# Two transformer blocks in one program: order of the first loads, halves of the output products, the router's choice, and the tail

## The chip, the cores and the metric

The kernel runs on one core of one Trainium2 chip. The metric is the device time of one execution in microseconds (us). Before the change three runs took 1857.16 us in the median (1853.68 to 1857.87).

## The reference

The program computes two blocks on 256 tokens of width 1024, all in fp32. `norm` is a root-mean-square norm, `ln` a layer norm.

```python
# first block
h = x
h = h + rglru_and_forgetting_attention(norm(h))       # w_in -> u, gate, q, k, v, f ; w_out
h = h + cross_attention(norm(h), norm(mem))           # 4 heads of 256, memory of 256
h = h + relu(norm(h) @ w_up) ** 2 @ w_down            # 1024 -> 4096 -> 1024
h = h + dilated_and_sliding_window_attention(norm(h)) # w_in -> qc, kc, vc, qd, kd, vd ; w_out
h = h + cross_attention(norm(h), norm(mem))
h = h + relu(norm(h) @ w_up) ** 2 @ w_down
x = norm(h)
# second block, twice (i = 0: f is latent attention, i = 1: f is a pooling mixer)
x = ln(a * x + f(x))
x = ln(a * x + moe(x))
# moe: the best of 8 groups of experts per token, in it the best 2 of 8 experts, gates by softmax
#   expert e: (silu(t @ w1[e]) * (t @ w3[e])) @ w2[e],  1024 -> 256 -> 1024, 64 experts
```

The kernel reads the weights of all 64 experts in both MoE layers (3 MB for each expert).

## The kernel before

**Products.** A product of the first block runs as three matmuls: both sides are split into a high part (`wh`, `yh`, by ScalarE) and a low part (`wl`, `yl`, by VectorE), and high·high, high·low and low·high are summed in PSUM. `split_steps` (L231, L234) splits a weight tile, `hilo` (L331, L332) an activation, `transposed` (L341 to L347) transposes x on TensorE and splits it on the way out of PSUM. `g_feat` (L301) makes a product by features: `mid` is called after its first weight half, `end` after its second, and `step` runs one step of the background work `bg` inside. `g_out` (L317) makes the products with an output matrix into four PSUM banks, for the token blocks b = 0 and 1.

**Weights.** All weights come over SyncE's queue (SP) in one list of items of about 1 MB, into a ring of buffers (13 more join for the MoE). `issue` starts loads as far ahead as the ring is free, `w` takes the next item and splits two further on, `tick` splits one half tile inside attention loops. Transfers of SP's queue run on eight lanes: a load waits for the one eight before it. The order of all other work is the order in which the Python text is executed; each engine works its queue in this order.

**First mixer (`mixer0`).** x is loaded by two DMAs, transposed, and multiplied to "u", "gate", then "vf", "kv" and so on. The row sums' scale `rs` (L356 to L372) is made in the middle of "u"; the products are multiplied by it as they leave PSUM (`evac`, L556). The recurrence `lru` is background work. Its small matrices `bd` come by four POOL DMAs (L551), `bf` by another (L540). `memory_start` transposes the memory (L341, L347).

**Attention.** `attend.main` loops over pairs of heads p: transposes of the probabilities (L470, L472), softmax of pair p+1, scores of p+2 (L712), `tick`, the output products of the pair before (`outp(p - 1)`, L317), the product with the values `pv` (L481) and its `hilo`. `cross` has a loop of the same form over four heads. `outl` is the output product of the recurrence's half.

**MoE (`moe`).** The choice of experts needs the logits `L` (L1318, L1322), two maxima with their indices (L1334, L1336), 0/1 masks `M` and counts by a triangular product (L1358). A gather (L1416) then builds the rows of four experts; `up` multiplies by w1 and w3 (L1452), `turned` transposes, `down` multiplies by w2 (L1481) and adds into the result by a gate matrix (L1490, `out`). 16 groups of four experts follow one another; w1, w3 and w2 of one expert are three items of 1 MB.

**End.** The last group (layer 1, group 15) takes w2 in four tiles of 256 columns for all four experts (`last`, L1511, L1504). `last_gain` broadcasts the final gain and bias (L1008), `finish` does the layer norm (L1023 to L1036) and the output (L1681, L1684) and stores it (L1685).

## Time and profile before

| what | value |
|---|---|
| median of the runs shown | 1857.16 us (1853.68 to 1857.87) |
| profiled execution | 1854.02 us, its span 1852.2 us |
| TensorE (PE) busy | 1649.1 us, 89% of the span |
| VectorE (DVE) busy | 760.0 us, 41% |
| ScalarE (ACT) busy | 577.7 us, 31% |
| GpSimd (POOL) busy | 10.2 us, 1% |
| read from memory | 546.97 MB, 296 GB/s over the span |
| mean granted TensorE clock | 0.964 |

The span is the time between the first and the last instruction of the profiled execution; 1.8 us lie around it. A busy share is a mean over stages. The first block takes the first 640 us and more, the latent attention ends at about 908 us, and the two MoE layers fill the rest.

### The profile page before, as it was taken

The page shows a single profiled execution, that of the slowest core. Times are in us where ns is not written, and L with a number is a line of the kernel's source. Part 1 is how long each engine was busy: PE and PEld are TensorE (multiplying, and loading weights), DVE is VectorE, ACT ScalarE, POOL GpSimd, SP SyncE. Part 2 cuts the span into 40 slices and gives each one's busy share as a digit, 9 for nine tenths or more (in the row PEclk, how much of TensorE's full clock was granted, in tenths as well). Part 3 has the DMA queues.
Part 4 walks back from the last instruction along what each step waited for, and adds up shares of the span by engine and source line. Part 5 has one row for each costly group of instructions (what it writes and reads, how often), then busy time and mean ns, then how long its engine had stood idle before and what let it go on. Part 6 is the DMA issues. An engine that isn't in the chain of part 4 may idle for free.

```text
span 1852.2 us, 29897 instructions
## 1 busy us (share of the span) xinstructions
PE 1649.1 (89%) x12712; PEld 1196.5 (65%) x12712; DVE 760.0 (41%) x1599; ACT 577.7 (31%) x1047; POOL 10.2 (1%) x22
## 2 busy tenths in 40 slices
...
GB/s 290 182 160 117 134 162 203 182 184 180 182 114 129 117 180 189 183 152 259 307 387 425 426 427 424 425 425 427 422 424 418 426 426 427 426 424 426 426 427 234
DMA packets 127842, 550.10 MB, mean 297 GB/s; under 512 B 9660, under 2 KB 33551, under 8 KB 78927
## 3 DMA queue, kind: packets, MB, share of 16 engines
...
q10 hardware_dynamic: 144, 0.21, 0.0%
HBM read 546.97 MB, written 1.05 MB: 296 GB/s over the span
## 4 chain that ended last, share of the span: by engine, by line
PE 54%; DMA 40%; DVE 3%; ACT 3%; issue 1%; SPq 0%; DVEq 0%; ACTq 0%
DMA wr<-in_moe_w 38%; PE a L317 16%; PE b L301 9%; PE a L301 4%; PE b L1452 4%; PE a L280 3%; PE b L741 3%; PE b L1416 2%; PE a L741 2%; DMA wr<-in_ab_w_in 1%; PE a L1490 1%; PE b L1481 1%; PE b L481 1%; PE b L470 1%; DVE wl L234 1%
## 5 line engine op out<-in xcount | busy, mean ns | idle before, releaser
L1452 PE MATMUL b<-wr,xg 128*32 128x256 f32 x4096 | 306.2, 422 | 111.2 <-DMA wr<-in_moe_w 108.9
L234 DVE TENSOR_TENSOR wl<-wr,wh 128x1024 fp32r<-128x1024 f32 (+4 forms) x268 | 309.5, 1197 | 120.8 <-ACT wh L231 77.2
L1452 PEld LDWEIGHTS b<-wr,xg 128*32 128x32 f32 x4096 | 145.0, 121 | 278.1 <-DMA wr<-in_moe_w 148.1
L231 ACT ACTIVATE wh<-wr 128x1024 fp32r<-128x1024 f32 (+4 forms) x268 | 265.1, 1037 | 106.4 <-DVE wl L234 72.4
L1457 DVE SCALAR_TENSOR_TENSOR th<-th,b 128x256 f32<-128x256 f32 x32 | 13.5, 421 | 487.2 <-ACT th L1456 487.2
L317 PE MATMUL a<-wh,yh 128*128 128x512 f32 x416 | 168.0, 404 | 2.7 <-ACT yh L331 2.7
L1456 ACT ACTIVATE th<-b 128x256 f32<-128x256 f32 x32 | 12.3, 383 | 506.3 <-PE b L1452 506.3
L317 PE MATMUL a<-wh,yl 128*128 128x512 f32 x416 | 165.1, 397 | 0.6 <-DVE yl L332 0.6
L317 PE MATMUL a<-wl,yh 128*128 128x512 f32 x416 | 164.1, 394 | 0.0
L1481 PE MATMUL b<-wr,hT 128*32 128x512 f32 x992 | 124.9, 603 | 28.8 <-ACT hT L1468 22.3
L1416 PE MATMUL b<-G,x 128*128 128x128 f32 x1024 | 130.0, 287 | 19.6 <-DVE G L1398 10.6
L1416 PEld LDWEIGHTS b<-G,x 128*128 128x128 f32 x1024 | 123.5, 200 | 33.1 <-issue 17.9
L301 PE MATMUL b<-xh,wl 128*128 128x256 f32 x448 | 121.9, 282 | 0.0
L301 PE MATMUL b<-xh,wh 128*128 128x256 f32 x448 | 121.7, 281 | 0.0
L1490 PE MATMUL a<-Y,GT 128*128 128x512 f32 x248 | 117.2, 615 | 0.0
L301 PE MATMUL b<-xl,wh 128*128 128x256 f32 x448 | 110.3, 282 | 0.0
L1481 PEld LDWEIGHTS b<-wr,hT 128*32 128x32 f32 x992 | 32.1, 110 | 100.7 <-issue 54.8
L317 PEld LDWEIGHTS a<-wh,yh 128*128 128x128 f32 x416 | 78.1, 188 | 23.3 <-ACT yh L331 4.5
L317 PEld LDWEIGHTS a<-wh,yl 128*128 128x128 f32 x416 | 78.1, 188 | 22.5 <-DVE yl L332 3.9
L1490 PEld LDWEIGHTS a<-Y,GT 128*128 128x128 f32 x248 | 42.0, 189 | 74.6 <-issue 30.5
L301 PE MATMUL a<-xh,wh 128*128 128x256 f32 x320 | 88.4, 286 | 1.3 <-ACT xh L345 0.9
L317 PEld LDWEIGHTS a<-wl,yh 128*128 128x128 f32 x416 | 78.2, 188 | 17.3
...
## 6 DMA issues: line engine op xcount, KB each, us to landing
wr<-in_moe_w SPq DMA_DIRECT2D x372, 1024.0 KB, 19.6
...
```

The lines of the kernel that those rows point to most:

```text
L231: nc.scalar.activation(hi[:, s], r[:, s], AF.Copy)
L234: nc.vector.tensor_tensor(lo[:, s], r[:, s], hi[:, s].bitcast(F32), op=ALU.subtract)
L280: nc.tensor.matmul(outs[b][j], xT(a, h * 4 + kk)[:, b * 128:(b + 1) * 128], wt[c][:, kk, j * n:(j + 1) * n], start=(h == 0 and kk == 0 and ...
L301: nc.tensor.matmul(o[f // 2][:, f % 2, :], wt[c][:, kk, f * 128:(f + 1) * 128], xT(a, h * 4 + kk), start=(h == 0 and kk == 0 and a == 0 an ...
L317: nc.tensor.matmul(acc[b][hf], yT[a][:, chunk, b * 128:(b + 1) * 128], wt[c][:, j, hf * 512:(hf + 1) * 512], start=(first and a == 0 and c ...
L470: nc.tensor.transpose(ps[:, o:o + 128], s[:, o:o + 128], self.ident)
L481: nc.tensor.matmul(o[r, sl], V(2 * p + e, kb), PT[p][e][:, 256 * kb:256 + 128 * kb], start=(kb == 0), stop=(kb == 1))
L741: nc.tensor.matmul(o[:, f], lt, rt, start=(k == 0 and f == 0 and a == 0 and c == 0), stop=(k == 7 and c == 1), skip_group_check=True)
L1416: nc.tensor.matmul(ps[:, k], xk[:, b, 4 * i + k], Gf[:, b], start=(b == 0), stop=(b == 1))
L1452: nc.tensor.matmul(ps[32 * e:32 * e + 32, which], xg[:, k, 32 * e:32 * e + 32], w(e, k), start=(which == 0 and k == 0), stop=(k == 7), ski ...
L1481: nc.tensor.matmul(y[hf][32 * e:32 * e + 32], hT[:, c, 32 * e:32 * e + 32], w(c)[:, hf * 512:(hf + 1) * 512], start=(c == 0), stop=(c == 1 ...
L1490: nc.tensor.matmul(acc[b][hf], GT[:, b * 128:(b + 1) * 128], Y[:, hf * 512:(hf + 1) * 512], start=first, stop=end, skip_group_check=True)
```

## The change

It has four parts.

1. Start: x comes in two halves of columns, the first weights between them; the rows of small vectors and the identity come over ScalarE's queue. `bf` and `bd` are loaded on SP, after the small vectors and ahead of the memory. The transposes of x are made in two parts, the second inside "u". `rs` is made at the end of "u", and its broadcast, the evacuation of u and the start of `lru` stand in the middle of "gate" (`scales`).
2. Output products: of the last pair, block 0's stand ahead of `pv` and block 1's behind it; the same by halves in `cross` and for `outl`; in the second mixer `turn("qd")` moves into the first pair.
3. Router: x is copied by ScalarE and VectorE, the expert is chosen in one 64-wide maximum over masked logits, the 0/1 matrices are bf16, and the first group gathers all rows ahead of its products, the gates ahead of them and the counts behind.
4. Tail: w3 of the last group comes in tiles of two experts by half of the rows, w2 in two tiles of two experts by 512 columns and two of four experts by 256; `last_gain` moves ahead by a group in layer 1; `finish` is divided over three engines.

```diff
         if self.w_split <= i or not self.attending:
-            self.split(i + (1 if i < 3 else 3 if key == ("lat", 1) else 2))
+            self.split(i + (0 if i == 0 else 1 if i < 3 else 3 if key == ("lat", 1) else 2))
...
+    def g_out(self, yT, chunk, wt, j, acc, first, last, blocks=(0, 1)):
         nc = self.nc
-        for b in range(2):
+        for b in blocks:
             for hf in range(2):
...
-                if p:
+                if p == n - 1:
+                    outp(p - 1, (0,))
+                elif p:
                     outp(p - 1)
                 elif pend:
                     pend()
                 if p == 0 and nxt:
                     follow = nxt()
                 pv(p)
+                if p == n - 1:
+                    outp(p - 1, (1,))
                 self.step()
...
-            xT = self.norm_in(R_AB, first)
+            xT = self.xt()
+            self.transposed(x, R_AB, xT, first, range(4))
+            for _ in first:
+                pass
+
+            def rest():
+                self.transposed(x, R_AB, xT, ks=range(4, 8))
+                yield
+            self.bg.append(rest())
...
-            nc.gpsimd.dma_start(bf, A["fox_b_f"].to_broadcast([128, 8]))
+            nc.sync.dma_start(bf, A["fox_b_f"].to_broadcast([128, 8]))
...
-                    nc.gpsimd.dma_start(bd[64 * e:64 * e + 64, i, :, 64 * e:64 * e + 64],
+                    nc.sync.dma_start(bd[64 * e:64 * e + 64, i, :, 64 * e:64 * e + 64],
...
-            o = self.g_feat(xT, "u", mid=lambda: self.rstd(x, None, out=rs))
-            rb, rbq = self.rbc(rs, (1.0, -0.125), "ab")
-            evac(upad[:, :, 3:259], o, rb)
-            self.bg.append(lru())
-            self.g_feat(xT, "gate", end=lambda o: evac(gate, o, rb))
+            ou = self.g_feat(xT, "u", end=lambda o: self.rstd(x, None, out=rs))
+            rbs = []
+
+            def scales():
+                rbs.extend(self.rbc(rs, (1.0, -0.125), "ab"))
+                evac(upad[:, :, 3:259], ou, rbs[0])
+                self.bg.append(lru())
+            self.g_feat(xT, "gate", mid=scales, end=lambda o: evac(gate, o, rbs[0]))
+            rb, rbq = rbs
...
-                if p % 2 == 0:
+            def outp(p, blocks=(0, 1)):
+                if p % 2 == 0 and 0 in blocks:
                     self.wo = self.w("ab_of", p // 2)
-                self.g_out(yb, p, self.wo, p % 2, acc, False, p == 3)
-
-            def outl(i):
-                wt = self.w("ab_ol", i)
-                for c in range(2):
-                    self.g_out(ya, 2 * i + c, wt, c, acc, i + c == 0, False)
-
-            outl(0)
-            last, _ = att.main(ahead=2)
-            outl(1)
+                self.g_out(yb, p, self.wo, p % 2, acc, False, p == 3, blocks)
+
+            def outl(i, c):
+                if c == 0:
+                    self.wl = self.w("ab_ol", i)
+                self.g_out(ya, 2 * i + c, self.wl, c, acc, i + c == 0, False)
+
+            outl(0, 0)
+            last, _ = att.main(pend=lambda: outl(0, 1), ahead=2)
+            outl(1, 0)
+            outl(1, 1)
             last()
             self.residual(x, acc)
...
                 self.tick(2)
                 if h:
-                    outp(h - 1)
+                    outp(h - 1, 0)
                 self.tick(2)
                 pv(h)
+                if h:
+                    outp(h - 1, 1)
             self.attending = False
             if before_last:
                 before_last()
-            outp(3)
+            outp(3, 0)
+            outp(3, 1)
             self.residual(x, acc)
...
-                turn("qd")
                 att0.pro(1)
                 self.attend_on()
             proj("vc", 0, mid)
...
-            fin, att1 = att0.main(nxt=swa)
+            fin, att1 = att0.main(pend=lambda: turn("qd"), nxt=swa)
...
+        zo = wp.tile([128, 2, 128], F32, name="hT", bufs=1).bitcast(BF16)
+        utb, onb = zo[:, 0, :128], zo[:, 1, :128]
+        i64 = small("i64", 64)
+        nc.gpsimd.tensor_copy(utb, self.ut)
+        nc.gpsimd.tensor_copy(onb, self.ones)
+        for i in range(2):
+            nc.gpsimd.tensor_scalar(i64[:, 32 * i:32 * i + 32], iota, 32.0 * i - 1.0, None, op0=ALU.add)
+        st, mv, r, u, rs, nb = self.norm_tiles(wp)
         for b in range(2):
-            for h in range(2):
-                nc.scalar.activation(half_x(b, h), by8(y[b][h]), AF.Copy)
+            nc.scalar.activation(half_x(b, 0), by8(y[b][0]), AF.Copy)
+            nc.vector.tensor_copy(half_x(b, 1), by8(y[b][1]))
+            if b == 0:
+                nc.vector.bn_stats(st[:, 0, 0], y[0][0])
+        for b in range(2):
...
+        self.norm_scales(2, st, mv, r, u, rs, nb)
+        for b in range(2):
+            stt(L[:, b], ps[:, b], rs[:, b:b + 1], self.lbr[:, l], op0=ALU.mult, op1=ALU.add)
...
+        gm, gi = largest("g", gl)
+        ne = small("ne", 2, 8)
+        Lm, o2 = (wp.tile([128, 256], F32, name=n, bufs=1)[:, :128].rearrange("p (b n) -> p b n", b=2) for n in ("th", "h"))
+        stt(ne, io8, -1.0, gi[:, :, 0:1].to_broadcast([128, 2, 8]), op0=ALU.add, op1=ALU.not_equal)
         for b in range(2):
...
+            stt(Lm[:, b].rearrange("p (g e) -> p g e", g=8), ne[:, b, :, None].to_broadcast([128, 8, 8]), -BIG,
+                L[:, b, 8:72].rearrange("p (g e) -> p g e", g=8), op0=ALU.mult, op1=ALU.add)
+        em, ei = largest("e", Lm)
+        o1 = small("o1", 2, 64)
+        M = wp.tile([128, 2, 64], BF16, name="r_M")
+        for j, o in enumerate((o1, o2)):
+            tt(o, i64[:, None, :].to_broadcast([128, 2, 64]), ei[:, :, j:j + 1].to_broadcast([128, 2, 64]), op=ALU.is_equal)
+        tt(M, o1, o2, op=ALU.add)
...
                     for e in range(4):
-                        it.append(((n, l, g, e), w[l, 4 * g + e].rearrange("(p k) f -> p k f", k=8), (8, 256)))
+                        if (l, g, n) == (1, 15, 3):
+                            it.append(((n, l, g, e), w[l, 4 * g + 2 * (e % 2):4 * g + 2 * (e % 2) + 2].rearrange(
+                                "e (p k) f -> p e k f", k=8)[:, :, 4 * (e // 2):4 * (e // 2) + 4], (2, 4, 256)))
...
-                        it.append(((2, l, g, e), A["moe_w2_2"][l, 4 * g:4 * g + 4].rearrange("e (p c) d -> p c e d", c=2)
-                                   [:, :, :, e * 256:(e + 1) * 256], (2, 4, 256)))
+                        es, ds = (slice(2 * e, 2 * e + 2), slice(0, 512)) if e < 2 else (slice(0, 4), slice(e * 256, (e + 1) * 256))
+                        it.append(((2, l, g, e), A["moe_w2_2"][l, 4 * g:4 * g + 4][es].rearrange("e (p c) d -> p c e d", c=2)
+                                   [:, :, :, ds], (2, es.stop - es.start, ds.stop - ds.start)))
...
+            def out(o, n):
+                for b in range(2):
+                    nc.tensor.matmul(acc[b][o // 512][:, o % 512:o % 512 + n], GT[:, b * 128:(b + 1) * 128],
+                                     Y[:, o:o + n], start=False, stop=True, skip_group_check=True)
+            wh = [self.raw_w(2, l, g, i) for i in range(2)]
+            hidden(0, 512, lambda c, e: wh[e // 2][:, c, e % 2])
+            for q in (2, 3):
+                w = self.raw_w(2, l, g, q)
+                hidden(q * 256, 256, lambda c, e: w[:, c, e])
+                out(*((0, 512) if q == 2 else (512, 256)))
+            out(768, 256)
...
-        Gg = []
-
-        def mid():
-            nonlocal G
-            gates()
-            half(1)
-            Gg.append(weighted(0, G))
-            G = slots(1, s1)
-        h = up(0, xg, parts(0), mid)
-        GT = back(Gg.pop())
+        half(1)
+        gates()
+        Gg = weighted(0, G)
+        G = slots(1, s1)
+        h = up(0, xg, parts(0))
+        rounds()
+        GT = back(Gg)
...
+            if g == 14 + (l == 0):
+                before_last()
             if g != OVER:
                 hT = turned(h)
             if 0 < g < 15:
                 GTn = back(Gg)
-            fill = []
-            if g == 15 and l == 0:
-                before_last()
-            if g == 14 and l == 1:
-                fill = [lambda i=i: before_last(i) for i in range(2)]
             if g != OVER:
-                down(g, hT, GT, acc, None if (l, g) == (1, 15) else w2g, g == 0, g == 15, fill)
+                down(g, hT, GT, acc, None if (l, g) == (1, 15) else w2g, g == 0, g == 15)
...
+        for j in range(4):
+            for b in range(2):
+                nc.vector.bn_stats(st[:, b, j], acc[b][j // 2][:, (j % 2) * 256:(j % 2 + 1) * 256])
+        self.norm_scales(4, st, mv, r, u, rs, nb)
+        o = [wp.tile([128, 1024], F32, name=n, bufs=1) for n in ("xg", "Y")]
+        h = slice(512, 1024)
+        nc.scalar.activation(o[1][:, h], acc[1][1], AF.Identity, scale=rs[:, 1:2], bias=nb[:, 1:2])
+        for i, op in ((0, ALU.mult), (1, ALU.add)):
+            nc.gpsimd.tensor_tensor(o[1][:, h], o[1][:, h], x[:, i, h], op=op)
+        for b, i in ((0, 0), (0, 1), (1, 0)):
+            s = slice(i * 512, (i + 1) * 512)
+            nc.vector.scalar_tensor_tensor(o[b][:, s], acc[b][i], mv[:, b, 0:1], x[:, 0, s], op0=ALU.subtract, op1=ALU.mult)
+            nc.vector.scalar_tensor_tensor(o[b][:, s], o[b][:, s], rs[:, b:b + 1], x[:, 1, s], op0=ALU.mult, op1=ALU.add)
+            nc.sync.dma_start(self.out[0, b * 128:(b + 1) * 128, s], o[b][:, s])
+        nc.scalar.dma_start(self.out[0, 128:, h], o[1][:, h])
...
-            nc.scalar.dma_start(keep, A["cst"][:, :C_KEEP])
-            nc.sync.dma_start(rows, A["rows"])
-            for b in range(2):
-                nc.sync.dma_start(x[:, b], A["x"][0, b * 128:(b + 1) * 128])
+
+            half = lambda h: nc.sync.dma_start(x[:, :, h * 512:(h + 1) * 512],
+                                               A["x"][0].rearrange("(b p) d -> p b d", p=128)[:, :, h * 512:(h + 1) * 512])
+            nc.scalar.dma_start(self.ident, A["cst"][:, C_ID:C_ID + 128])
+            nc.scalar.dma_start(rows, A["rows"])
+            half(0)
+            self.issue(0)
+            half(1)
+            self.issue(self.depth)
             nc.vector.memset(self.ones, 1.0)
             nc.scalar.activation(self.junk[:, :2], self.ones[:, :2], AF.Copy)
             nc.gpsimd.memset(self.brow, 0.0)
             nc.gpsimd.memset(self.bsrow, 0.0)
-            self.issue(1)
+            nc.sync.dma_start(keep[:, 128:], A["cst"][:, 128:C_KEEP])
             nc.sync.dma_start(cst, A["cst"][:, C_KEEP:])
-            self.issue(self.depth)
```

Three places show the order in the queues. VectorE's queue in the first products: `rb` is the broadcast scale, `upad` holds u, `wl` are the low parts of weights, `lc` begins the constants of the recurrence, `rs` is the scale. Before:

```order
L372 SCALAR_TENSOR_TENSOR rs<-nwt,nwy 128x2
L234 TENSOR_TENSOR wl<-wr,wh 128x1024 x2
L382 TENSOR_SCALAR rb_341<-b 128x256
L382 TENSOR_SCALAR rb_343<-b 128x256
L556 TENSOR_TENSOR upad<-a,rb_341 128x2x256 x2
L234 TENSOR_TENSOR wl<-wr,wh 128x1024 x2
L562 TENSOR_SCALAR lc<-col 128x8
```

and now:

```order
L377 SCALAR_TENSOR_TENSOR rs<-nwt,nwy 128x2
L239 TENSOR_TENSOR wl<-wr,wh 128x1024 x2
L387 TENSOR_SCALAR rb_400<-b 128x256
L387 TENSOR_SCALAR rb_402<-b 128x256
L573 TENSOR_TENSOR upad<-a,rb_400 128x2x256 x2
L579 TENSOR_SCALAR lc<-col 128x8
L414 SCALAR_TENSOR_TENSOR l1e<-col 128x4
```

The evacuation of u stood between the low parts of the first half of "gate" and those of its second; now it stands behind both. Four `wl` of 128x1024 (the second half of "u" and the first of "gate") stand ahead of the scale where two did.

TensorE's queue at the first group of layer 0, from the end of the triangular product on; `G` gathers, `xg` are the gathered rows, `r_M` the 0/1 matrix of the counts. (An fp32 product is counted once here and twice in the trace.) Before:

```order
L1358 MATMUL b<-r_M,keep 128x64
L1416 MATMUL b<-G,x 128x128 x8
L1452 MATMUL b<-wr,xg 32x256 x16
L1386 MATMUL b<-r_M,ones 128x64 x2
L1416 MATMUL b<-G,x 128x128 x8
L1452 MATMUL b<-wr,xg 32x256 x48
```

and now:

```order
L1411 MATMUL b<-r_M,hT 128x64
L1465 MATMUL b<-G,x 128x128 x16
L1497 MATMUL b<-wr,xg 32x256 x64
L1436 LDWEIGHTS hT
L1436 MATMUL b<-r_M,hT 128x64
```

The second half of the gather stood between the first 16 up products and the other 48; now the whole gather stands ahead of all 64, and the product of the counts behind them.

TensorE's queue at the end of the program, from the turn of the last group on. Before:

```order
L1466 MATMUL b<-keep,h 128x128 x2
L1511 MATMUL b<-wr_19715,hT 32x256 x8
L1511 MATMUL b<-wr_19718,hT 32x256 x8
L1504 MATMUL a<-Y,GT 128x256 x2
L1511 MATMUL b<-wr_19749,hT 32x256 x8
L1504 MATMUL a<-Y,GT 128x256 x4
L1511 MATMUL b<-wr_19752,hT 32x256 x8
L1504 MATMUL a<-Y,GT 128x256 x2
```

and now:

```order
L1510 MATMUL b<-keep,h 128x128 x2
L1544 MATMUL b<-wr_19698,hT 32x512 x2
L1544 MATMUL b<-wr_19701,hT 32x512 x2
L1544 MATMUL b<-wr_19698,hT 32x512 x2
L1544 MATMUL b<-wr_19701,hT 32x512 x2
L1544 MATMUL b<-wr_19732,hT 32x256 x8
L1550 MATMUL a<-Y,GT 128x512 x2
L1544 MATMUL b<-wr_19735,hT 32x256 x8
L1550 MATMUL a<-Y,GT 128x256 x4
```

The w2 products of the first 512 columns are now eight 512-wide ones over two tiles, and fewer output products (`Y`, `GT`) stand behind the last weights.

## Rows read from the trace of the kernel before

**Rows 1.** The page's slices of 46 us: what the DMA engines moved.
```profile
GB/s 290 182 160 117 134 162 203 182 184 180 182 114 129 117 180 189 183 152 259 307 387 425 426 427 424 425 425 427 422 424 418 426 426 427 426 424 426 426 427 234
```

**Rows 2.** The page's chain that ended last, by engine and line.
```profile
DMA wr<-in_moe_w 38%; PE a L317 16%; PE b L301 9%; PE a L301 4%; PE b L1452 4%; PE a L280 3%; PE b L741 3%; PE b L1416 2%; PE a L741 2%; DMA wr<-in_ab_w_in 1%; PE a L1490 1%; PE b L1481 1%; PE b L481 1%; PE b L470 1%; DVE wl L234 1%
```

**Rows 3.** Stretches: us, busy of PE, PEld, DVE, ACT, POOL, clock, DMA share, GB/s.
```profile
14.00:22.00 8.00, 7.71 (x62) 7.38 (x62) 7.43 (x16) 7.97 (x17) 0.00 (x0) 1.00 1.05 397
14.00:48.00 34.00, 31.88 (x252) 30.48 (x252) 31.31 (x76) 23.21 (x41) 0.00 (x0) 1.00 0.87 303
129.00:168.00 39.00, 37.62 (x223) 28.94 (x222) 25.19 (x85) 17.70 (x50) 0.00 (x0) 1.00 0.33 109
199.00:238.00 39.00, 37.45 (x180) 30.11 (x179) 18.15 (x29) 17.10 (x33) 0.00 (x0) 1.00 0.41 131
238.00:512.00 274.00, 273.74 (x1789) 248.65 (x1789) 169.50 (x235) 128.84 (x173) 1.25 (x2) 1.00 0.56 183
512.00:572.00 60.00, 58.71 (x348) 43.83 (x347) 40.35 (x144) 37.19 (x107) 0.00 (x0) 1.00 0.28 95
602.00:638.00 36.00, 34.53 (x158) 26.93 (x157) 16.34 (x23) 12.65 (x23) 0.00 (x0) 1.00 0.30 99
925.00:930.00 5.00, 4.45 (x57) 3.13 (x60) 3.65 (x19) 0.91 (x2) 0.00 (x0) 1.00 0.49 205
930.00:935.00 5.00, 5.00 (x79) 3.44 (x71) 1.05 (x4) 0.66 (x2) 0.00 (x0) 1.00 0.82 290
950.00:1357.00 407.00, 324.15 (x2992) 168.38 (x2984) 60.12 (x116) 37.77 (x87) 0.00 (x0) 0.93 1.01 425
1405.00:1415.00 10.00, 9.02 (x127) 5.88 (x125) 4.07 (x15) 2.03 (x5) 0.00 (x0) 1.00 0.97 392
1812.00:1818.00 6.00, 5.23 (x34) 3.02 (x35) 0.00 (x0) 0.00 (x0) 0.00 (x0) 0.50 1.02 420
1820.00:1830.00 10.00, 10.00 (x111) 5.53 (x104) 0.68 (x2) 1.58 (x3) 0.00 (x0) 1.00 1.00 335
```

**Rows 4.** ScalarE at the start: start us, us, engine line op [idle before <-releaser].
```profile
12.72 0.63 ACT L231 ACTIVATE wh<-wr 128x512 fp32r<-128x512 f32 x1 [10.07 <-DMA wr<-in_ab_w_in]
```

**Rows 5.** VectorE in the start, same columns.
```profile
27.20 1.28 DVE L556 TENSOR_TENSOR upad<-a,rb 128x512 f32<-128x512 f32 x2
44.95 3.22 DVE L347 SCALAR_TENSOR_TENSOR yl<-b,col,yh 128x256 fp32r<-128x256 f32 x8
```

**Rows 6.** TensorE, the last product of vf.
```profile
55.29 0.40 PE L280 MATMUL a<-wh,xl 128*128 128x260 f32 x2
```

**Rows 7.** DMA issues: engine, count, KB each, median us to landing.
```profile
wr<-in_moe_w SPq DMA_DIRECT2D x8, 512.0 KB, 13.0
bd<-in_lru_w_a POOLq DMA_DIRECT2D x2, 64.0 KB, 9.7
```

**Rows 8.** SyncE's queue, one small load.
```profile
24.56 0.44 SPq L1750 DMA_DIRECT2D pcol<-in_ln_g  x1
```

**Rows 9.** ScalarE, the copies of x in the MoE of layer 0.
```profile
906.57 3.77 ACT L1310 ACTIVATE x<-a 128x512 f32<-128x512 f32 x4 [1.05 <-PE a L317]
```

**Rows 10.** TensorE, first group of experts of layer 0.
```profile
920.35 2.02 PE L1416 MATMUL b<-G,x 128*128 128x128 f32 x16 [0.93 <-DVE G L1398]
927.98 5.48 PE L1452 MATMUL b<-wr,xg 128*32 128x256 f32 x96 [0.55 <-ACT xg L1424]
```

**Rows 11.** TensorE, the last part of w1's products, and the last product.
```profile
1812.77 3.62 PE L1452 MATMUL b<-wr,xg 128*32 128x256 f32 x26 [1.86 <-DMA wr<-in_moe_w]
1838.90 1.13 PE L1504 MATMUL a<-Y,GT 128*128 128x256 f32 x4 [0.50 <-ACT Y L1513]
```

**Rows 12.** VectorE in the tail.
```profile
1839.63 1.52 DVE L1023 BATCH_NORM_STATS2 bst<-a 128x6 f32<-128x256 f32 x4 [1.97 <-PE a L1504]
1843.52 1.40 DVE L1681 SCALAR_TENSOR_TENSOR xg<-a,bmv,x 128x512 f32<-128x512 f32 x2
```

**Rows 13.** POOL, its largest fill.
```profile
1.98 0.97 POOL L548 MEMSET bd<- 128x1024 f32 x1
```

179 lines of the change are left out of this document (79 added, 100 removed).

## The prediction

> **What bounds the kernel now.** I read the slices of the span first, then the chain that ended last, then the busy time in stretches, and last the start and the end instruction by instruction.
>
> The rate of the transfers splits the program in two [rows 1]. In the first 19 slices (a slice is 46 us) it lies between 114 and 290 GB/s; from the 22nd to the last but one it stands at 418 to 427. The chain says the same: 38% of the span is the landing of expert weights, and the rest is nearly all TensorE [rows 2]. The stretches give the two regimes in numbers [rows 3]. From 238 to 512 us TensorE works 273.74 of 274 us: there, time is TensorE's own work plus its stalls. From 950 to 1357 us the DMA share is 1.01 at 425 GB/s while TensorE is busy for 324.15 of 407: there, and in the same way in the second layer's MoE, nothing that an engine does counts, only the bytes, which the change leaves alone.
>
> So there are three places to win. A stall of TensorE before about 925 us shifts all that follows, since the weight stream can fill only as many buffers as have been used. A hole in the stream where the MoE begins (205 and 290 GB/s in 925 to 935) is lost for good. And what follows the last weights at about 1812 us is a chain by itself.
>
> The profiled execution took 1854.0 us (span 1852.2); I sum against that. The median of the runs shown is 3.1 higher.
>
> **The start.** Before, the first split waits 10.07 us for the first piece of weights, at 12.72 [rows 4]. The new order puts half of x ahead of that piece, not the rows and all of x: 0.57 MB less. At about 270 GB/s (near the 303 of [rows 3]) this is 2 us, and 4 where the first transfers also queue less. But VectorE is the next limit: it is busy 31.31 of the 34 us from 14 to 48 [rows 3], and TensorE 31.88 of them. In the new order the row sums' scale is made inside "gate", so the evacuation of u (1.28) comes about 6 us (half of a 12 us product) after the end of u, right behind which it stood before (27.20); all that stood after it (the little recurrence's constants, the evacuation of gate, the eight memory subtractions at 44.95 of 3.22 in all) [rows 5] comes after it still. Counting those and the four weight splits of 1.2 us each between them behind the later evacuation, the products "vf" end 1 to 2 us earlier than the 55.7 of before (55.29+0.40) [rows 6]: an estimate, between 0.5 for a start that VectorE eats and 2 for one that passes through. I take 1.5. Bounds: 4.5 if VectorE does not bind, −1 if the scale's wait stops the queue behind it (the splits for "gate" stand there, and TensorE waits for them).
>
> The four loads of lru_w and that of b_f go from POOL's queue into SP's, ahead of the memory and "vf" weights. As issues they are 0.44 us each, like the small vector's load that SP already issues at 24.56 [rows 8], some 2.2 us in front of transfers that land late anyway; I put them inside the bounds above. On POOL the lru_w loads took 9.7 us to land [rows 7]; that price returns as a rival.
>
> **Output products in halves.** In the first mixer's attention, in both cross-attentions and in the second mixer the last stages had a product whose left side was not ready. The idle time of TensorE in these four stretches is 39.00−37.62 = 1.38, 39.00−37.45 = 1.55, 60.00−58.71 = 1.29 and 36.00−34.53 = 1.47 us [rows 3]. The change puts six to twelve products (0.4 us of busy time each, pipelined) between the evacuation and its user, more than any one of these waits. I take all 5.7. The cover is the other half of the output products; if it is gone, the stall comes back entire, not more. From below: 2.5, if only the cross-attentions profit, since the second mixer's moved turn brings a pair of splits forward in queues that are already full there (VectorE 40.35 of 60). From above 8: ends of matmuls are modelled, so the idle times undercount a stall.
>
> **Router and first group of experts.** The copies of x take 3.77 us on ScalarE one after another [rows 9]; shared by two engines, the second block's are done 1.9 earlier, of which the statistics, now queued behind VectorE's two copies, eat about half: 1.0. The choice on 64 columns has 0.1 fewer, the 0/1 products in 2-byte form 0.3. The bigger part is order. Before: gather half (920.35), 32 products, gather half, and 96 products from 927.98 on, 5.48 long, of which the first third still uses w1: those buffers are free at 927.98+1.83 = 929.8 [rows 10]. After: two halves of the gather (2.0 each from 920.35), then 64 products in one run of 3.7: 928.1. Together 1.0+0.1+0.3+1.7 = 3.1. The ceiling is what the stream loses there: (425−205)/425×5 + (425−290)/425×5 = 4.2 us. In the second layer it loses only (425−392)/425×10 = 0.8 [rows 3], which I count in full: 3.9 for both. From below: 1.5, if the gates, which now stand ahead of the first product, hold VectorE's evacuation of the gathered rows.
>
> **The tail.** After the last w1, TensorE runs at a granted clock of 0.50 from 1812 to 1818 (1.2 GHz, of its two levels 1.2 and 2.4) [rows 3]; it does the last 26 up products of w1 there (from 1812.77, after a wait of 1.86 [rows 11]) and the gain's broadcast, and is still at work on w3 when w2 arrives. The change puts the broadcast a group earlier, so that these products are done before the wait, not after it, and lets half of w3 and half of w2 be used as they land. The landing is then the bound: 8.4 MB behind 1812.8 at 425 GB/s is 19.7 us, 1832.5, less what the longer runs of two of the w2 tiles give (2.1 MB at 425 and not 335 [rows 3]: 1.3 us): 1831.2. Behind it are 8 products (1.1), a copy (0.5) and two products (0.6): 1833.4, where the last ones began at 1838.90 and took 1.13 [rows 11], so 1840.0. That is 6.6; w2's landing will not be that smooth and TensorE not always at the full clock, and I take 5. Bounds: 2.5 (half clock again) and 6.6.
>
> Then the norm. Two of the four statistics of the last block are left behind the last product (1.52/4 each), and a half costs 2×0.70 [rows 12]: 0.75 less. VectorE does three halves of the output, not four: 1.4 less. The fourth half goes over ScalarE and two POOL operations of 128x512. No POOL operation of two inputs is in this trace; the nearest is a fill of 128x1024 in 0.97 us [rows 13], so 0.5 each from below; from above, 2.5 each before it would cost anything more than it saves. VectorE needs 4.2 for its halves, and the branch has 4.2−0.6 = 3.6 for the two. I take 1.5 for the finish (0 to 2.1).
>
> The Trainium skill, "GPSIMD Engine Reference", section 3.1 (Elementwise — side-by-side cycle accounting), speaks against that branch: two-input elementwise there costs about 2.6 cycles for each element against one on VectorE. From its 4497 ns for 2048 elements an estimate for 512 is 1.1 us, so 2.2 for both, inside the 3.6; by this page the sum stays.
>
> **The sum.** 1.5+5.7+3.9+5+1.5 = 17.6; 1854.0−17.6 = 1836.4, so 1836.
>
> **The rivals.**
> 1. The front gives nothing: VectorE's chain eats the earlier start and the waits in the attention parts only move to the next user, as TensorE's queue is in order and its left sides come at the pace of ScalarE. For it: VectorE at 92% in the start. Against: VectorE is busy for 16.34 of 36 us in the second cross-attention. 1854.0−(3.9+6.5) = 1843.6, so 1844.
> 2. The start gains in full (4.5) and the stalls cost their modelled ends too (8): 1854.0−(4.5+8+3.9+6.5) = 1831.
> 3. The tail's pieces are slower. All w3 now goes in transfers of 512 KB, as w2 did before; the 335 GB/s of 1820 to 1830 belongs to transfers of 512 KB with 1 KB runs (eight of them [rows 7]), and the trace does not tell which of the two made it. If it is the size, 4.2 MB of w3 at 335 take 2.7 us more and w2's longer runs give nothing: the tail falls from 6.5 to about 2.5, and the time is 1840. Against: transfers of 2 KB runs at the start move 397 GB/s [rows 3], so the run may be what counts.
> The Trainium skill, "DMA: Bandwidth & Descriptors", section Bandwidth, has a rule on this side: gather transfers to 1 MiB or more, below that the rate falls. By that rule the result would be rival 3.
> 4. Slower. The five small loads stand in SP's queue, ahead of the memory, "vf" and every later weight, and a transfer of this queue starts only after an earlier one on its lane has landed. If each of the four loads of lru_w takes its 9.7 us [rows 7] in series and not side by side, all behind comes 38.8 us later, and the time is 1854.0+38.8−17.6 = 1875. It decides from two such landings in series (19.4). Against: the small loads that already stand in SP's queue there cost an issue of 0.44 us [rows 8], and there are eight lanes.
>
> **How the numbers follow.** Forecast 0.6; rival 1: 0.15; rival 2: 0.1; rival 3: 0.1; rival 4: 0.05. The forecast's own range is 1830 to 1842. With rivals 2 and 3 and part of 1 the range is 1829 to 1846. A measurement of this kernel tells 0.2%, 3.7 us, from no change. All cases but the fourth are faster by more than that; a few hundredths go to a sum of lower bounds (−1+2.5+1.5+2.5+0 = 5.5) with something lost beside: faster 0.92, same 0.03, slower 0.05.
>
> **What would show it.** First main product at 9 to 11 us and "vf" ended at 53.5 to 55 if the start is right; idle TensorE under 0.4 us in each of the four attention stretches; first gather 1.4 us earlier relative to the last MLA product, and 10 us from there on with no rate below 350 GB/s; granted clock 1.0 in the last 40 us and the last output product 21 us behind the last w1; POOL's two operations over before VectorE's third half. I am wrong if TensorE's idle time of the first 640 us stays as it was, if small loads stand in the stream for more than 5 us, or if w3's pieces land at 335 GB/s.

## The result, and the profile after

The changed kernel took 1839.93 us in the median (four runs, 1839.08 to 1842.37), the kernel before in the same rounds 1855.72 (1853.68 to 1857.87): a ratio of 0.992 with a 95% interval of 0.9905 to 0.9935, so 15.8 us faster. The forecast was 1836 with a range of 1829 to 1846. The profiled execution took 1839.1 us (span 1837.3), 14.9 less than that of before. All sums below are on these two traces; most runs of experiments are single executions, so I read them by stage and not by their total.

The gain by stages, read from the start of the same TensorE work in both traces (the transposes of each norm, the last product) and, where the weight stream sets the pace, from the time at which the same number of bytes of weights is still to land (the output, stored behind the last product, is not counted):

| stage | predicted | measured |
|---|---|---|
| start, up to the first mixer's attention | 1.5 | 0.7 |
| output products in halves, four stretches | 5.7 | 8.0 |
| router and first group of experts, two layers | 3.9 | 3.7 |
| tail, to the last product | 5 | 1.9 |
| finish | 1.5 | 0.6 |
| sum | 17.6 | 14.9 |

First stretches of after, in the columns of [rows 3].

```profile
14.00:22.00 8.00, 7.33 (x62) 7.12 (x61) 7.22 (x17) 7.88 (x11) 0.00 (x0) 1.00 0.85 279
...
129.00:168.00 39.00, 37.85 (x220) 28.65 (x218) 25.28 (x87) 17.83 (x50) 0.00 (x0) 1.00 0.33 107
196.00:236.00 40.00, 39.62 (x200) 33.24 (x201) 22.35 (x39) 19.23 (x34) 0.00 (x0) 1.00 0.44 139
...
508.00:568.00 60.00, 58.94 (x347) 43.52 (x346) 41.41 (x146) 37.82 (x109) 0.00 (x0) 1.00 0.29 98
596.00:632.00 36.00, 35.72 (x178) 29.74 (x177) 18.91 (x28) 15.29 (x29) 0.00 (x0) 1.00 0.37 124
916.00:921.00 5.00, 5.00 (x100) 3.03 (x96) 2.95 (x14) 0.31 (x2) 0.00 (x0) 1.00 0.94 342
921.00:926.00 5.00, 3.40 (x38) 2.46 (x34) 2.88 (x10) 1.88 (x5) 0.00 (x0) 1.00 1.02 423
...
1800.00:1806.00 6.00, 6.00 (x56) 2.75 (x60) 0.69 (x1) 0.00 (x0) 0.00 (x0) 1.00 0.89 335
...
1812.00:1818.00 6.00, 3.45 (x40) 1.61 (x44) 1.02 (x2) 0.77 (x2) 0.00 (x0) 1.00 1.00 352
```

Against [rows 3]: TensorE idles 0.38 us in the first cross-attention where it idled 1.55, and 0.28 in the second where it idled 1.47, but still 1.15 in the first mixer (1.38 before) and 1.06 in the second (1.29 before). The first group of experts, 205 and 290 GB/s before, now runs at 342 and 423. In these stretches of the tail the granted clock is 1.00, but the stream is at 335 and 352 GB/s (375 between them) and not at 425.

ScalarE's first split in after, which answers [rows 4]; it waits 2.85 us for the first weights where it waited 10.07:

```profile
6.01 0.63 ACT L236 ACTIVATE wh<-wr 128x512 fp32r<-128x512 f32 x1 [2.85 <-DMA wr<-in_ab_w_in]
```

TensorE's waits in the start of after (start us, us, engine line op, idle before it and what ended it):

```profile
39.31 0.39 PE L285 MATMUL a<-wh,xh 128*128 128x260 f32 x1 [3.13 <-DVE gate L573]
39.91 0.59 PE L285 MATMUL a<-wh,xh 128*128 128x260 f32 x1 [0.21 <-DVE gate L573]
45.04 1.10 PE L604 MATMUL b<-tu,bd 128*128 128x256 f32 x4 [1.18 <-DMA wr<-in_xa_w_kv]
```

The first main product begins at 7.80 (before 13.76), 6 us earlier, and 4.5 us of it go in these waits: "vf" must have a PSUM buffer that VectorE frees by evacuating gate, and VectorE first has u, the constants of the recurrence and its first steps to do. Two rows of VectorE show what is late:

```profile
28.10 0.76 DVE L387 TENSOR_SCALAR rb<-b 128x256 f32<-128x256 f32 x2 [3.65 <-PE b L383]
...
43.96 3.22 DVE L352 SCALAR_TENSOR_TENSOR yl<-b,col,yh 128x256 fp32r<-128x256 f32 x8
```

Ahead of the scale `rb` VectorE stands idle for 3.65 us, because the product that broadcasts it waits in TensorE's queue in the middle of "gate". The row at 45.04 names a DMA; its operand `tu` was finished at 41.74. It starts 1.08 us behind the first of the memory's subtractions (43.96), in after as in three runs of experiments in which these stand elsewhere, so it is most likely they that free its PSUM buffer. "vf" ends at 55.62; before it ended at 55.69.

First group of layer 0, and the tail, on TensorE:

```profile
910.68 3.81 PE L1465 MATMUL b<-G,x 128*128 128x128 f32 x32 [0.94 <-DVE G L1447]
914.42 7.11 PE L1497 MATMUL b<-wr,xg 128*32 128x256 f32 x128
...
1803.56 5.80 PE L1497 MATMUL b<-wr,xg 128*32 128x256 f32 x98
1809.87 0.62 PE L1497 MATMUL b<-wr,xg 128*32 128x256 f32 x2 [0.52 <-DMA wr<-in_moe_w]
1811.12 0.62 PE L1497 MATMUL b<-wr,xg 128*32 128x256 f32 x2 [0.62 <-DMA wr<-in_moe_w]
...
1815.93 0.41 PE L1510 MATMUL b<-keep,h 128*128 128x128 f32 x2 [1.66 <-DVE h L1503]
...
1820.21 0.64 PE L1544 MATMUL b<-wr,hT 128*32 128x256 f32 x8 [0.63 <-DMA wr<-in_moe_w]
1820.78 1.98 PE L1550 MATMUL a<-Y,GT 128*128 128x512 f32 x4
1822.70 1.07 PE L1544 MATMUL b<-wr,hT 128*32 128x256 f32 x16
1823.70 1.99 PE L1550 MATMUL a<-Y,GT 128*128 128x256 f32 x8
```

Against [rows 10] the gather is one run and the 128 records of up products follow without a wait. Against [rows 11] the wait for w1 is gone from the tail; each short wait for a DMA is now for a piece of w3 or w2 that has just landed.

The finish of after, VectorE, POOL and ScalarE's part (L1738 reads PSUM and one tile in SBUF, L1739 two tiles in SBUF):

```profile
1825.30 1.53 DVE L1729 BATCH_NORM_STATS2 n_st<-a 128x6 f32<-128x256 f32 x4 [1.40 <-PE a L1550]
...
1829.13 0.74 DVE L1738 SCALAR_TENSOR_TENSOR xg<-a,n_mv,x 128x512 f32<-128x512 f32 x1
1829.33 0.78 ACT L1733 ACTIVATE Y<-a,n_nb,n_rs 128x512 f32<-128x512 f32 x1 [5.11 <-DVE n_nb L1329]
1829.91 0.75 DVE L1739 SCALAR_TENSOR_TENSOR xg<-xg,n_rs,x 128x512 f32<-128x512 f32 x1
1830.19 3.26 POOL L1735 TENSOR_TENSOR Y<-Y,x 128x512 f32<-128x512 f32 x2 [479.90 <-ACT Y L1733]
1830.58 0.74 DVE L1738 SCALAR_TENSOR_TENSOR xg<-a,n_mv,x 128x512 f32<-128x512 f32 x1
...
1831.36 0.97 DVE L1739 SCALAR_TENSOR_TENSOR xg<-xg,n_rs,x 128x512 f32<-128x512 f32 x1
1832.26 0.74 DVE L1738 SCALAR_TENSOR_TENSOR Y<-a,n_mv,x 128x512 f32<-128x512 f32 x1
1833.03 0.97 DVE L1739 SCALAR_TENSOR_TENSOR Y<-Y,n_rs,x 128x512 f32<-128x512 f32 x1
```

The same operation of VectorE before the change, with two tiles in SBUF and no POOL operation beside it, took 0.74 for each:

```profile
1844.84 1.41 DVE L1684 SCALAR_TENSOR_TENSOR xg<-xg,brs,x 128x512 f32<-128x512 f32 x2
```

As in [rows 12] four statistics (1.53) stand behind the last product. From the last product's end to the end of the span it is 11.6 us, before 12.2.

### The profile page after: what moved, and what is told of

It reads as the page before. It is cut to its first block, busy times and chain, and to the rows that moved or that the text cites. A ratio compares the mean times of both kernels' runs of the same rounds, so it can differ in the third digit from the quotient of the medians.

```text
span 1837.3 us, 29848 instructions
## 1 busy us (share of the span) xinstructions
PE 1645.4 (90%) x12682; PEld 1200.0 (65%) x12682; DVE 763.4 (42%) x1582; ACT 576.6 (31%) x1043; POOL 12.5 (1%) x27
## 4 chain that ended last, share of the span: by engine, by line
PE 50%; DMA 45%; DVE 3%; ACT 2%; issue 1%; SPq 0%; ACTq 0%; DVEq 0%
DMA wr<-in_moe_w 44%; PE a L322 16%; PE b L306 9%; PE a L306 6%; PE a L285 3%; PE b L763 3%; PE a L763 2%; PE b L1497 2%; PE b L486 1%; PE b L1465 1%; PE b L475 1%; PE b L346 1%; PE b L801 1%; DMA wr<-in_xa_w_kv 1%; PE b L734 1%; PE b L828 1%
## 5 line engine op out<-in xcount | busy, mean ns | idle before, releaser
L1497 PEld LDWEIGHTS b<-wr,xg 128*32 128x32 f32 x4096 | 148.9, 122 | 272.9 <-DMA wr<-in_moe_w 146.4
```

Source lines behind the costliest of these rows:

```text
L1497: nc.tensor.matmul(ps[32 * e:32 * e + 32, which], xg[:, k, 32 * e:32 * e + 32], w(e, k), start=(which == 0 and k == 0), stop=(k == 7), ski ...
```

## The experiments

Each is the changed kernel with one edit. "Against after" means against the changed kernel's trace at the same TensorE work; "against the stream" means that the lead or lag of the weights, at the same number of bytes still to land, is taken off.

### What holds the start

**Small loads behind the first weights.** The 17 small loads (constants, router rows, `bf`, `bd`) go behind the memory and the "vf" weights (shortened).

```diff
-            nc.sync.dma_start(bf, A["fox_b_f"].to_broadcast([128, 8]))
-                    nc.sync.dma_start(bd[64 * e:64 * e + 64, i, :, 64 * e:64 * e + 64],
...
             ou = self.g_feat(xT, "u", end=lambda o: self.rstd(x, None, out=rs))
+                    nc.sync.dma_start(bd[64 * e:64 * e + 64, i, :, 64 * e:64 * e + 64],
+            nc.sync.dma_start(bf, A["fox_b_f"].to_broadcast([128, 8]))
+            self.late()      # the other twelve, which stood at the start of the queue
```

> The changed kernel with the small loads (constants from the second part on, rows of the later norms, router weights, lru_w, b_f) put in SP's queue behind the memory and the two vf weights instead of ahead of them. Measured in the changed kernel: the evacuation of gate at 38.58 us, the first wait of TensorE on it 3.13 us, the last product of vf ended at 55.6. Theory A (VectorE's queue is what is late, since the scale is made in the middle of gate): the low parts of the first vf tile lose only their 0.68 us of idle time, the gate evacuation starts at about 37.9, vf ends 0.5 to 0.8 us earlier. Theory B (the vf weights land late behind the small loads, ScalarE idle 2.84 us for them): vf ends 2.5 us earlier or more.

1841.4 us (before beside it 1856.85). Neither number came: "vf" ended at 57.18, 1.6 later than after. The wait for gate was still there:

```profile
39.02 1.18 PE L285 MATMUL a<-wh,xh 128*128 128x260 f32 x2 [2.58 <-DVE gate L568]
```

and the stretches behind it, in the columns of [rows 3], were

```profile
40.00:44.00 4.00, 4.00 (x19) 3.80 (x18) 3.93 (x6) 2.49 (x4) 0.00 (x0) 0.50 1.09 363
44.00:48.00 4.00, 3.36 (x12) 2.93 (x12) 3.79 (x15) 1.18 (x3) 0.00 (x0) 0.50 0.65 231
```

ScalarE split the weights of "vf" 2.5 us earlier (30.81, after 33.27), and still TensorE waited for gate: the loads alone do not hold "vf". Behind the wait the granted clock stood at 0.50 for 10.2 us, where after had 3.4; that is why the run cannot tell what the earlier weights are worth.

**The scale ahead of "gate".** `scales()` runs before the products of gate, and the background step behind gate's last half is left out, so that gate is evacuated first.

```diff
-            self.g_feat(xT, "gate", mid=scales, end=lambda o: evac(gate, o, rbs[0]))
+            scales()
+            self.g_feat(xT, "gate", end=lambda o: evac(gate, o, rbs[0]))
...
-                if k == 2:
+                if k == 2 and (key, h) != ("gate", 1):
```

> The changed kernel with the broadcast of the scale, the evacuation of u and the start of the recurrence ahead of gate again, as before the change (one background step inside gate left to its end, so that the gate evacuation stands ahead of the second convolution). Theory A (VectorE's queue): its 3.65 us of idle time ahead of the scale at 28.10 goes, the gate evacuation starts at about 36.7, the wait of 3.13 us falls to 1.3, and vf ends 1.5 to 2 us earlier than 55.6. Theory B (landing of vf): vf weights land at 33.3 as now, gate evacuation behind their low parts, vf ends at most 0.5 us earlier.

1837.72 us. "vf" ended at 52.88, 2.7 earlier than after, more than Theory A's 2; the wait for gate fell from 3.13 to 0.21 and the clock stayed at 1.00 through the start. A wait of 2.60 came in front of the recurrence's products instead (42.33). About 1.5 us were lost again in the second mixer, where this execution had a half-clock stretch of 3.4 us (mean 0.72 in 520 to 526) that after does not have. The order in VectorE's queue is shown as the cause; what the scale's place and the left-out step give apart is not.

**Both:** the scale first and the small loads late, most of them one place later than above, behind the memory's key weights (shortened).

```diff
+            scales()
+            self.g_feat(xT, "gate", end=lambda o: evac(gate, o, rbs[0]))
...
+            self.late()
```

> Follows from the two runs on the start: the scale ahead of gate moved the end of vf from 55.6 to 52.9 us, and the late small loads alone moved it to 57.2, with TensorE at half clock for 10 us behind its wait on gate. Here both: scale ahead of gate, the memory and vf weights ahead of the small loads, lru_w and b_f right behind these, and the rest of the small loads behind the memory's key weights, so that these are not delayed either. Theory A+B (VectorE's queue first, and once that is mended the landing of vf at 32.4 us is late): the low parts of vf start at about 32.5 not 33.55, no wait on gate, and vf ends at 51.5 to 52.3. Rival A alone (queue only; the next bound is the memory's subtraction that frees a bank for the recurrence's products): vf ends at 52.7 or later.

1839.18 us (before 1853.42): "vf" ended at 54.17, worse than with the scale alone, with a half-clock stretch of 3.4 us at 42. This is the rival's side (52.7 or later); no gain from late small loads is seen.

**The scale first, and one split moved.** As with the scale ahead of "gate" above, and at the weight item with index 4 the splits run one item ahead and not two, so that two splits come later in the queues (the expectation of the timed run below calls this "one more split").

```diff
-            self.split(i + (0 if i == 0 else 1 if i < 3 else ...
+            self.split(i + (0 if i == 0 else 1 if i < 3 or i == 4 else ...
```

> The changed kernel with the scale ahead of gate (as in the run that ended vf at 52.9 us), and the memory's subtractions ahead of the low parts of the second vf tile on VectorE. In that run TensorE waited 2.60 us for the first of these subtractions, which frees a bank for the recurrence's products. Theory A (VectorE's queue order sets the start): that wait falls under 0.5 us, no idle time over 0.7 us is left between 8 and 56 us, and vf ends at 50 to 51. Rival: VectorE's work as a sum is the limit (it is busy nearly without a gap from 20 to 50 us), the wait turns up at the second half of vf, and vf ends at 52 or later.

1837.36 us: "vf" ended at 51.96, and the wait at the recurrence's products is 0.30, where it was 2.60 with the scale alone. The wait fell as Theory A had it; the end came between its 50 to 51 and the rival's 52.

**TensorE kept busy in the wait.** 13 products with the identity ahead of "vf".

```diff
+            for _ in range(13):
+                nc.tensor.matmul(o[0][0][:, :128], self.ident, self.ident, start=True, stop=True)
```

> The changed kernel with 13 identity products of 128x128 ahead of vf, into a bank that vf then starts anew, so that TensorE works through its wait of 3.13 us for the evacuation of gate. They compute nothing that is used. In seven profiles with the same start the granted clock fell to 0.50 at 39 to 41 us for 3.4, 6.8 or 10.2 us, and vf ended between 55.6 and 58.7. Theory K (TensorE's idle time there takes the clock down, and that costs 1.7 us or more on top of the wait): no stretch at 0.50 before 60 us, vf ends at 53.8 to 54.4. Rival (the clock falls for another reason, the wait itself is the price): the clock falls again, vf ends at 55.5 or later.

1841.97 us. The clock stayed at 1.00 through the start, and "vf" still ended at 56.02 (after 55.62): the time moved into the next wait for VectorE's chain.

```profile
39.72 0.39 PE L285 MATMUL a<-wh,xh 128*128 128x260 f32 x1 [0.39 <-DVE gate L573]
...
45.45 1.10 PE L604 MATMUL b<-tu,bd 128*128 128x256 f32 x4 [2.60 <-DMA wr<-in_xa_w_kv]
```

So in after it is VectorE's queue and not the clock that holds the start; a short half-clock stretch lies inside that wait, a long one does not. This execution lost 1.5 us elsewhere, in a half-clock stretch of 3.4 us at 526.

### The halves

**Whole output products again,** in all four stretches.

```diff
-                if p == n - 1:
-                    outp(p - 1, (0,))
-                elif p:
+                if p:
                     outp(p - 1)
...
+                turn("qd")        # back to its old place; cross and outl whole too
```

> The changed kernel with the output products undivided again in all attention parts and cross-attentions, and the turn of qd back in the middle of vc; start, router and tail as in the change. The idle time of TensorE counted before was 5.7 us in four stretches; the traces show the latent attention's last product 8.7 us earlier after the change, 0.8 of it from before the first attention. Theory E (stalls cost more than their idle time, all 7.9 us come from the halves): it ends 7.9 us later than in the changed kernel, at about 907.8, and the time is about 1847. Rival: the halves give their idle time only, 5.7, and it ends at 905.6.

1849.77 us: the latent attention's last product came 8.1 us later than after, 0.3 of it from before the first attention; the rest is Theory E's 7.9, not the rival's 5.7, and the stream came 8.0 later from there to the last 8 MB. Behind them the run lost 2.7 more, with a half-clock stretch of 10.2 us in the tail, whose code is that of after. What a stall costs beyond its idle time stands in the starts of the products. Second cross-attention, one stage of before and the same of after:

```profile
612.68 0.60 PE L798 MATMUL b<-keep,xs 128*128 128x128 f32 x4
613.53 0.50 PE L317 MATMUL a<-wh,yh 128*128 128x512 f32 x1 [0.25 <-ACT yh L331]
613.87 0.39 PE L317 MATMUL a<-wl,yh 128*128 128x512 f32 x1
614.26 0.50 PE L317 MATMUL a<-wh,yl 128*128 128x512 f32 x1
614.60 0.40 PE L317 MATMUL a<-wh,yh 128*128 128x512 f32 x1
```

```profile
607.21 0.60 PE L820 MATMUL b<-keep,xs 128*128 128x128 f32 x4
607.56 0.48 PE L322 MATMUL a<-wh,yh 128*128 128x512 f32 x1
607.88 0.40 PE L322 MATMUL a<-wl,yh 128*128 128x512 f32 x1
608.11 0.39 PE L322 MATMUL a<-wh,yl 128*128 128x512 f32 x1
608.34 0.39 PE L322 MATMUL a<-wh,yh 128*128 128x512 f32 x1
```

From the turn to the fourth product it is 1.92 us before and 1.13 after: 0.79 for a stall of which the idle column shows 0.25. A product's row is 0.40 long while the next starts 0.23 behind it, so a row overlaps the first part of each wait.

**The turn of "qd" at its old place.**

```diff
+                turn("qd")
                 att0.pro(1)
...
-            fin, att1 = att0.main(pend=lambda: turn("qd"), nxt=swa)
+            fin, att1 = att0.main(nxt=swa)
```

> The changed kernel with the turn of qd back in the middle of vc, all output products in halves as in the change. In the changed kernel the first pair waits 0.89 us for the turned qd; the second mixer with the norm behind it became 2.1 us shorter (from a shift of 3.4 to 5.5 us), 1.7 of it in the first products behind the norm, whose weights were split a step earlier. Theory F (the moved turn lets one more weight tile be split inside the attention): the 1.7 us are lost again, the wait for the turned qd goes, and the end of the second mixer's following projection comes 1 to 2 us later. Rival G (the halves did it): 0 to 0.7 us earlier than in the changed kernel.

1843.14 us. The second mixer became 0.5 shorter (its wait for ScalarE's `qdT`, 0.89 in after, became one of 0.81 for `pt`), but two waits of 0.38 and 0.87 for the weight splits came back in the norm's first products behind it, and from there on all came 1.8 later against the mixer's end. The move pays 1.3 us, one stage after the place where it was made.

### The router

**The gather in two halves again,** around the first up products, with the rest of the change in the router left in.

```diff
-        half(1)
-        gates()
-        Gg = weighted(0, G)
-        G = slots(1, s1)
-        h = up(0, xg, parts(0))
+        h = up(0, xg, parts(0), mid)      # mid: gates, half(1), weighted, slots
```

> The changed kernel with the first group's gather in two halves again, the second between the halves of the w1 products, and the gates there; the rest of the router as in the change. Between the end of the latent attention and the steady stream the change had gained 3.65 us in layer 0 and 0.65 in layer 1. Theory H (order of the first group frees the w1 buffers earlier): the stream loses 1.5 to 2 us of the 3.65 and 0.3 to 0.6 in layer 1, the time is 2 us longer. Rival (the router's shorter chain does it): the stream loses less than 0.5 us in layer 0.

1843.99 us. TensorE was 2.0 us late when the MoE began (a half-clock stretch of 10.2 us in the start), the stream 3.7 after its first group, and 3.7 after that of the second layer: the order is worth 1.7 us in layer 0, as Theory H had it, and nothing in layer 1. The other 1.3 and 0.7 are left for the router's chain, which no run takes apart.

### The tail

**w3 as whole tiles of 1 MB.**

```diff
-                        if (l, g, n) == (1, 15, 3):
-                            it.append(((n, l, g, e), ... [:, :, 4 * (e // 2):4 * (e // 2) + 4], (2, 4, 256)))
```

> The changed kernel with w3 of the last group in whole experts of 1 MB again (runs of 8 KB), w2 as in the change. Measured in the changed kernel: from 1800 to 1808 us the stream moved 320 to 350 GB/s, the last product ended at 1825.7, its group's w3 products at 1814.3. Theory C (the pieces of 512 KB slow the stream): 400 GB/s or more in that stretch, the last weights land 1.5 to 2 us earlier, the last product ends 1.5 to 2 us earlier (span about 1835.4 where the rest runs alike). Theory D (the wait is TensorE's own: half of w3 used early is worth more than the rate): the w3 products end 1 us later or more and the last product no earlier than now.

1843.11 us, stretches from 1800 on:

```profile
1800.00:1806.00 6.00, 4.54 (x54) 1.98 (x56) 0.00 (x0) 0.00 (x0) 0.00 (x0) 1.00 1.02 422
1806.00:1812.00 6.00, 2.98 (x28) 0.78 (x17) 0.00 (x0) 0.00 (x0) 0.00 (x0) 0.92 0.81 316
1812.00:1818.00 6.00, 4.58 (x44) 2.18 (x48) 0.00 (x0) 0.00 (x0) 0.00 (x0) 0.51 0.89 309
```

With whole tiles w3 lands at 422 GB/s instead of 335, and the stream is 0.9 us ahead of after's with 4 MB of weights left (it was 0.5 behind when w3 began), but w2 gives it back: the last packet comes 1.0 behind. The last 8 MB took 25.0 us, as with the pieces (24.5 in after, 24.3 to 25.4 in the eleven other runs that have them). The Trainium skill, "DMA: Bandwidth & Descriptors", section Bandwidth, asks for transfers of 1 MiB or more; the rate of w3 agrees, the end of the stream comes no sooner. TensorE waited 1.2 to 1.8 us for each tile and then worked at the half clock, so its last product came 3.3 us later against the stream. That the small pieces are the better choice because TensorE is on time with them is likely, not shown: it is one execution, and with the pieces too a long half-clock stretch cost 2.7 us in one (whole output products).

**Output products behind each half of w2,** as early as they can run.

```diff
-                hidden(q * 256, 256, lambda c, e: w[:, c, e])
                 out(*((0, 512) if q == 2 else (512, 256)))
+                hidden(q * 256, 256, lambda c, e: w[:, c, e])
```

> The changed kernel with the output products of the first 512 columns ahead of the products of the third w2 tile, and those of the next 256 ahead of the fourth's. In the changed kernel TensorE waits 0.15 and 0.63 us for the third tile's halves and then does 1.98 us of output products while the fourth lands (last packet at 1822.5); the last product ends at 1825.7. Theory I (the last landing is the bound, 1.1 us of products, a copy of 0.4 and 1.0 us of output products behind it): the last product ends 0.7 us earlier relative to the last landing. Rival J (TensorE's own work is the bound): 1.3 us earlier, the work done while it waits.

1848.6 us. The start had 10.2 us at half clock (some 3 us late by the MoE), and the tail 3.4 and 6.8 us:

```profile
46.00:50.00 4.00, 4.00 (x18) 3.73 (x17) 3.65 (x16) 1.33 (x3) 0.00 (x0) 0.50 0.52 185
...
1825.00:1830.00 5.00, 4.25 (x12) 1.31 (x12) 0.46 (x2) 0.60 (x1) 0.00 (x0) 0.52 0.02 8
```

The last product came 6.4 us later against the stream. Both theories were of the order of the products; the clock decided, and it is not known whether the edit caused the stretches in the tail or this execution had them anyway.

**TensorE kept busy in the tail:** identity products between the pieces of w3 and behind w1's.

```diff
+                        if which and k == ks[0] and e:
+                            fill(spare, 2)      # two products with the identity
...
+            fill(spare, 7)
```

> The changed kernel with identity products in TensorE's waits of the last group: two ahead of each of the first expert's successors in each part of w3, seven behind the last one. They compute nothing that is used. In the profiles so far the granted clock in the last 25 us of products was 1.0 throughout in three and fell to 0.50 for 3.4 to 10 us in the others, where the end of the last product stood 3 to 6 us later against the stream of weights. Theory K (idle time of TensorE takes the clock down): no stretch at 0.50 between 1795 us and the last product, which ends 25.9 us or less behind the point where 8 MB are left to land, as in the changed kernel's profile. Rival: the clock falls in the same way.

1842.06 us. The start was 2.4 us late (first product 0.66 later, a half-clock stretch of 3.4 us at 46). The tail kept its clock:

```profile
1815.00:1820.00 5.00, 5.00 (x50) 3.39 (x48) 1.03 (x2) 0.38 (x1) 0.00 (x0) 1.00 0.94 327
1820.00:1825.00 5.00, 4.47 (x39) 1.82 (x38) 0.09 (x1) 1.37 (x3) 0.00 (x0) 1.00 0.51 178
```

But its last product was 0.6 us later against the stream than in after, which kept its clock without the extra products. Runs with after's tail code lost 0.2 to 0.8 us there at full clock (late small loads, best version, turn back) and 0.2 to 1.0 with a half-clock stretch of 3.4 us (scale first, 13 products in the start, both). It is no gain that these runs can show.

### The best version, timed

> The same code as s8 (the changed kernel with the scale ahead of the gate in the first layer, one background step less behind the gate and one more split), now timed in five rounds beside the kernel before, to see whether it beats both. Theory A (the first layer's wait for the gate is what holds TensorE, and with the scale first it goes, in nearly every execution): median 1836.5 to 1838.5, ratio to the kernel before 0.990 to 0.991, against 0.992 for the changed kernel, with executions spread over less than 2.5 us, since a full-speed start takes away the half-speed stretch of 3 to 10 us that the changed kernel's executions had there. Rival L (the one execution of s8 was a lucky one, in which TensorE kept its clock through the start): median 1839 to 1841, spread 3 us or more, and a half-speed stretch at 36 to 50 us in the profiled execution.

1837.12 us in the median of four runs (1835.77 to 1837.24) against 1854.03 of before (seven runs, 1853.40 to 1855.49): a ratio of 0.9906, interval 0.9889 to 0.9922. The four runs lie within 1.5 us, those of the changed kernel within 3.3. All three numbers are Theory A's. "vf" ends at 52.62 at a clock of 1.00:

```profile
38.00 0.39 PE L285 MATMUL a<-wh,xh 128*128 128x260 f32 x1 [0.99 <-DVE gate L573]
...
41.43 1.10 PE L604 MATMUL b<-tu,bd 128*128 128x256 f32 x4 [0.29 <-PE a L285]
```

The medians are 2.8 us apart, and the stream of the profiled execution comes 2.5 us earlier than in after. But the kernel before was 1.7 us faster beside these runs too, so against it the gain is 16.9 where the changed kernel's was 15.8, and the two intervals overlap: that the version beats the changed kernel is likely, not certain.

## Why the prediction was right, and where it was not

The forecast was right in sign and held in its range: the measured gain is 15.8 us where 17.6 were forecast. That it came so near is in part luck. The term of the halves was 2.3 us too small and the other four together 5.0 too large. Rival 3's time was 1840, with 2.5 us for tail and finish, and 2.5 is what these two gave. Of the prediction's own signs, the clock of the last stretches came; an idle TensorE under 0.4 us came in two of the four stretches; the rate behind the first gather fell to 342 GB/s, a little under its 350; and w3's pieces did land at 335 GB/s, which it had named as a sign of being wrong.

**Start, 1.5 predicted, 0.7 measured.** The bound was right (VectorE's queue holds "vf"), the first product even earlier than the 9 to 11 forecast; but VectorE stood idle for 3.65 us ahead of the scale, so that the evacuation of u began at 28.77, later than the 27.20 of before, and "vf" ended at 55.62, 0.1 earlier and outside 53.5 to 55. The other 0.6 of the stage came behind "vf", where no run was aimed. The step that failed is the estimate that the products "vf" end 1 to 2 us earlier. The scale first gave 2.7 us at "vf", 3.0 in the timed version.

**Small loads on SP.** Rival 4 did not come: the four loads of `bd` land 2.2 to 2.4 us after their issue (9.7 from POOL's queue) and side by side. The stream does drop to 157, 156, 65 and 119 GB/s in the four stretches of 2 us from 18 to 26, which is more than the 5 us that the prediction named as a sign of being wrong. ScalarE waits 2.84 us for the "vf" weights that are late by it (33.27), but late small loads gave no earlier "vf".

**Halves, 5.7 predicted, 8.0 measured.** The cover held in the cross-attentions (2.5 and 2.8 gained), not in the mixers (some 0.2 in the first and nothing in the second; 1.8 came in the norm behind the second, by the turn's move; 0.5 in the last pair of the latent attention, which has the same loop; the rest spreads over the stages). The size is that of the upper bound, not of the idle times: in the cross-attentions 1.17 and 1.19 us of idle time less gave 2.5 and 2.8, and in the pair of views above a stall of 0.25 cost 0.79. "If it is gone, the stall comes back entire, not more" was wrong in "not more".

**Router, 3.9 predicted, 3.7 measured.** Order 1.7 (1.7 predicted), chain 1.3 (1.4), layer 1 0.7 (0.8). The first gather came 0.95 us earlier against the last product of the latent attention, not 1.4; the rest of the chain's part fell behind it.

**Tail, 5 predicted, 1.9 measured.** This step failed: "The landing is then the bound: 8.4 MB behind 1812.8 at 425 GB/s". Before, 7.0 MB were left to land at 1812.8, as 1.4 MB of w3 had come in beside the end of w1, and these took 21.7 us, 322 GB/s; the last 7.0 MB of after took 21.9. The prediction's landing, 1831.2, lies 3.2 us ahead of the 1834.4 of before; against the stream the measured one is 0.5 later (the lead of 12.4 us fell to 11.9). On the way w3's pieces lost 1.5 (335 GB/s in 1800 to 1806, rival 3's mechanism) and the bytes from 5 to 1.2 MB left gave 1.1 back, near the 1.3 that the prediction had from w2's longer runs. But with w3 whole the same w2 tiles gave nothing back: these bytes took 11.8 us there, 11.3 before and 10.2 in after. In no run with the new tiles did the last 8 MB take less than the 24.0 us of before. Why the end of the stream keeps its length no run here settles; a lead is that in 1800 to 1806 the DMA share is 0.89, while it is 1.02 with whole tiles.

Behind the last packet (1834.44 before, 1822.55 after) TensorE's work shrank from 5.6 to 3.1 us; the prediction had 2.2. It counted two output products and two statistics there, but `out(512, 256)` stands behind the last tile's products as well, so there are four of each. So the full clock came and less work stands behind the landing, as forecast; the landing did not come sooner. The prediction's reading of [rows 11] is off too: the 26 records are 13 products of w1's first half, and the 32 records of its second half run behind them, at 1819.25.

**Finish, 1.5 predicted, 0.6 measured.** All four statistics still stand behind the last product, not two. POOL's two operations took 1.59 us each (the estimate beside the forecast was 1.1), 3.26 with the gap between them of the 3.6 that the branch had; but while they ran, VectorE's operation with two inputs in SBUF took 0.97, where it took 0.74 before the change and 0.75 when it was begun before POOL's; the one that reads PSUM stayed at 0.74. VectorE's six operations took 4.9 us from the first to the last, the eight of before 5.4. The Trainium skill, "GPSIMD Engine Reference", section 1 (Specifications), says that GpSimd shares its SBUF interfaces with VectorE and that they contend when VectorE has two SBUF inputs; these rows agree.
